# Two-layer encoder trunk on one core: twelve-tile down projections by single column groups, and the last two steps of each pair group by group

## The chip, the cores and the metric

One core of a Trainium2 chip runs the whole program. The time is that of one execution on the device in microseconds, and the lower one is the better one. TensorE (PE in the profile) multiplies, its weight loads (PEld) overlap the multiplications, VectorE (DVE) and ScalarE (ACT) do the element-wise work, GpSimd (POOL) does a little of it elsewhere in the program, and SyncE's queue (SP) issues the loads of the weights.

## The reference

256 tokens of 2048 features go through two layers. Layer 0 mixes the tokens with grouped-query attention, layer 1 with a recurrent block. Behind each mixer stands a feed-forward part, which this change is about:

```
def swiglu(h, w_gate, w_up, w_down):
    return (jax.nn.silu(h @ w_gate) * (h @ w_up)) @ w_down
...
        x = x + mix
        x = x + swiglu(rms_norm(x, norm_ffn[i]), ffn_w_gate[i], ffn_w_up[i], ffn_w_down[i])
```

`w_gate` and `w_up` are 2048 x 5632, `w_down` is 5632 x 2048, and all is float32.

## The kernel before, in words

**Products.** A float32 operand is split into a high part (`hi`, rounded to the format that TensorE takes at full rate) and a low part (`lo`, the rest). One product of tiles is three matmuls: high by high, high by low and low by high. A matmul here multiplies 128 tokens (there are two token halves, `a`) by 512 columns over 128 rows of the weights.

**Weights.** All weights of the feed-forward part stream through `load_half` (line 109): 512 KB, that is 256 rows by 512 columns, are loaded into `raw`, ScalarE casts them to `hi` (line 122) and VectorE subtracts to get `lo` (line 123). Each of the three tags has five buffers. `ffn_order` (line 137) lists the halves in the order in which TensorE takes them, and `half` (line 162) hands out the next.

**Tiles and parts.** The 5632 hidden features are 44 tiles of 128. `PARTS` (line 28) deals them out in three parts of 12, 16 and 16 tiles. For each part `ffn` (line 760) runs the units, each of which makes four hidden tiles, and then the down projection of this part, which adds to the residual `x_tok`. So a layer has 3 + 4 + 4 units and three down projections.

**Pairs.** Both are made of calls of `project_pair` (line 276). A pair computes two column groups of 512 at once, gate and up for a unit, two neighbouring groups of the output for a down projection (which so has two pairs, `c` of 0 and 2). A pair holds four accumulators, two groups by two token halves, and these are all four buffers of the pool `ps_a`. It goes through steps of two row tiles each, eight steps for sixteen tiles and six for twelve. In a plain step the first group's half is taken and multiplied (12 matmuls), then the second group's (12 matmuls).

**Seven-product steps.** Two steps of each pair, listed in `SEVEN` (line 29), use a scheme of the Strassen kind: seven products in place of eight, so 21 matmuls in place of 24. It needs sums of the weights (`seven_forms`, line 245: four VectorE additions at lines 252 to 255, a cast at 259 and a split at 260), sums of the tokens' operand (`x_forms`, line 264), four more accumulators in the pool `ps_m`, and after the last such step `merge` (line 317), which works these accumulators into two tiles `fg` and `fu`. The order of the steps is in `USUAL_STEPS` and, for the first unit of a layer, `FIRST_STEPS` (lines 30 and 31).

**After a pair.** A unit adds the accumulators to `fg` and `fu` (lines 766 and 769), applies SiLU to the gate (line 526, by way of a helper), multiplies (line 770), and `turned` (line 444) turns the result by two VectorE transposes (line 448) and sixteen ScalarE copies (line 456). The four hidden tiles are then cast and split (lines 775 and 776). A down pair adds `fg` and `fu` to `x_tok` (line 500), then the accumulators (line 509), and in the last part of layer 0 `norm.add` (line 410) then prepares the operands of the next norm, column by column (lines 412, 448, 454, 456, 404 and 405). In the last part of layer 1 the columns are stored.

**Single groups.** The output projections of attention and of the recurrence are done by `output` (line 476) and `project_tokens` (line 223): one column group at a time, two accumulators, plain steps only, one half of weights (12 matmuls, line 235) per step, and adds to `x_tok` at line 484.

**Order.** TensorE's instructions run in the order in which the program is written. Those of the other engines are ordered by a planner, which picks among what is ready by the order of the program and its own estimate of times; each engine then keeps that order.

Of the kernel before, what the change touches and what calls it, by code (L numbers as in the profile page):

```python
# [14 lines left out]
AF = mybir.ActivationFunctionType  # L15
# [10 lines left out]
NBLK = 8  # L26
DFF = 5632
PARTS = [12, 16, 16]
SEVEN = {6: (1, 3), 8: (2, 5)}
USUAL_STEPS = {6: (0, 2, 1, 4, 3, 5), 8: (0, 1, 2, 3, 4, 5, 6, 7)}  # L30
FIRST_STEPS = (0, 1, 3, 4, 2, 6, 5, 7)
HALF = 8
WIDE = 512
NCOL = D // WIDE
# [38 lines left out]
def trunk(ctx, tc, w, out):  # L73
# [56 lines left out]
    def wide(name):  # L130
        src = w[name]
        return [(src[c, i], HALF) for c in range(src.shape[0]) for i in range(src.shape[1])]

    def pair_steps(n, first=False):
        return FIRST_STEPS if first else USUAL_STEPS[n]

    def ffn_order(l):
        units = [wide(f"w_gate{l}"), wide(f"w_up{l}")]
        seq, i = [], 0
        for p, n in enumerate(PARTS):  # L140
            for _ in range(n // FOUR):
                for k in pair_steps(KT // 2, i == 0):
                    seq += [u[i + k] for u in units]
                i += KT // 2
            down = wide(f"w_down{l}_{p}")
            for c in range(0, len(down), n):
                for k in pair_steps(n // 2):
                    seq += [down[c + k], down[c + n // 2 + k]]
        return seq

    order = [(w["w_k"][i], HALF) for i in range(len(KEY_TILES))]
# [90 lines left out]
    def flat(t):  # L242
        return t.rearrange("p (k c) f -> p k (c f)", k=2)
# [29 lines left out]
        dve.tensor_tensor(t[:, 1], y[:, 4:, :], t[:, 0].bitcast(F32), ALU.subtract)  # L273
        return [(t[:, 0, i, :], t[:, 1, i, :]) for i in range(4)]

    def project_pair(xs, forms, middle, first=False):
        banks = [[new_acc() for _ in range(2)] for _ in range(2)]
        begun = set()

        def product(acc, x, wt, last=False):  # L280
            for i, (a, b) in enumerate(((x[0], wt[0]), (x[0], wt[1]), (x[1], wt[0]))):
                pe.matmul(acc, a, b, start=id(acc) not in begun, stop=last and i == 2)  # L282
# [7 lines left out]
        steps = pair_steps(len(xs) // 2, first)  # L290
        seven = [n for n in steps if n in forms]
        for n in steps:
            if n in forms:
                s1, s2, s3, s4 = forms[n]
                b11, b21, t3, b22, t1, t2, t4 = seven_forms()
                if n == seven[0]:
                    p1, q6, q5, q7 = (ps_m.tile([P, WIDE], F32, tag="pm", name=nm("pm")) for _ in range(4))
                last = n == seven[-1]
                product(p1, tokens(2 * n, 0), b11, last)
                product(banks[0][0], tokens(2 * n + 1, 0), b21)  # L300
                product(banks[1][0], s4, b22)
                product(q7, s3, t3, last)
                product(q5, s1, t1, last)
                product(q6, s2, t2, last)
                product(banks[0][1], tokens(2 * n + 1, 1), t4)
                if last:
                    middle(p1, q5, q6, q7)
            else:
                for j in range(2):
                    half()  # L310
                    hi, lo = (flat(t) for t in newest["tiles"])
                    for a in range(2):
                        for k in range(2):
                            product(banks[j][a], tokens(2 * n + k, a), (hi[:, k, :], lo[:, k, :]), n == steps[-1] and k == 1)
        return banks

# [74 lines left out]
    class Norm:  # L391
# [18 lines left out]
        def add(self, c):  # L410
            for a in range(2):
                act.activation(tmp("nj", (P, WIDE), bufs=1), x_tok[:, a, c, :], AF.Square, accum_out=self.sums[:, a, c : c + 1])
            for f in turned(x_tok[:, :, c, :]):
                self.operand(f, True)
            for n in SEVEN[KT // 2] if self.seven else ():
# [60 lines left out]
    def output(xs, norm=None, end=False, ready=0, close=None):  # L476
        for c in range(NCOL):
            accs = project_tokens(xs, ready, None if c else close)
            for a, acc in enumerate(accs):
                n = 2 if end and c == NCOL - 1 else 1  # L480
                for i in range(n):
                    sl = slice(i * WIDE // n, (i + 1) * WIDE // n)
                    y = x_tok[:, a, c, sl]
                    dve.tensor_tensor(y, y, acc[:, sl], ALU.add)
                    if end:
                        sync.dma_start(out=out[:, a, c, sl], in_=y)
            if norm is not None:
                norm.add(c)
        if norm is not None:
            norm.finish()  # L490


    def down(xs, forms, norm=None, end=False):
        for c in (0, 2):
            def middle(*banks):
                g, u = merge(*banks)
                for j, t in enumerate((g, u)):
                    for a in range(2):
                        y = x_tok[:, a, c + j, :]
                        dve.tensor_tensor(y, y, t[:, a, :], ALU.add)  # L500

            banks = project_pair(xs, forms, middle)
            for j in range(2):
                for a in range(2):
                    n = 2 if end and c + j == NCOL - 1 else 1
                    for i in range(n):
                        sl = slice(i * WIDE // n, (i + 1) * WIDE // n)
                        y = x_tok[:, a, c + j, sl]
                        dve.tensor_tensor(y, y, banks[j][a][:, sl], ALU.add)  # L509
                        if end:  # L510
                            sync.dma_start(out=out[:, a, c + j, sl], in_=y)
                if norm is not None:
                    norm.add(c + j)
        if norm is not None:
            norm.finish()

# [8 lines left out]
    def table_act(*a, **k):  # L525
        table_op(act.activation(*a, **k))
# [231 lines left out]


    def ffn(norm, nxt):  # L760
        def unit(hid, forms, seven, first):
            got = []
            banks = project_pair(norm.xs, norm.forms, lambda *banks: got.extend(merge(*banks)), first)
            g, u = got
            for a, acc in enumerate(banks[0]):
                dve.tensor_tensor(g[:, a, :], acc, g[:, a, :], ALU.add)
                table_act(g[:, a, :], g[:, a, :], AF.Silu, scale=norm.rt[:, a : a + 1])
            for a, acc in enumerate(banks[1]):
                dve.tensor_tensor(u[:, a, :], acc, u[:, a, :], ALU.add)
                dve.scalar_tensor_tensor(u[:, a, :], u[:, a, :], norm.rt[:, a : a + 1], g[:, a, :], ALU.mult, ALU.mult)  # L770
            first = len(hid)
            for f in turned(u, False):
                h = act_tile()
                hi, lo = (h[:, o : o + S].rearrange("p (q t) -> p q t", t=32) for o in (0, S))
                act.copy(hi, f)  # L775
                dve.tensor_tensor(lo, f, hi.bitcast(F32), ALU.subtract)
                hid.append(h)
            for i, n in enumerate(seven):
                if first <= 2 * n < len(hid):
                    forms[n] = x_forms(hid[2 * n], hid[2 * n + 1], f"hf{i}")  # L780

        for p, n in enumerate(PARTS):
            hid, forms = [], {}
            for i in range(n // FOUR):
                unit(hid, forms, SEVEN[n // 2], p == i == 0)
            last = p == len(PARTS) - 1
            if last and nxt is not None:
                ln_exp_tables()
            down(hid, forms, nxt if last else None, last and nxt is None)

    nr = Norm("norm_mix", KT)
    ffn(nf, nr)
# [218 lines left out]
```

## Time and profile before

| | us |
|---|---|
| median of 3 runs | 2042.35 |
| lowest and highest | 2038.47 and 2043.43 |
| profiled execution, its own time | 2042.2 |
| its span, from the first to the last instruction | 2040.4 |
| mean granted TensorE clock | 0.990 |

The profile's times are those of one execution. Its page gives busy times by engine and the costliest groups of instructions, each with the line of the kernel, the operation, the tiles written and read, the count, the busy time and mean duration, and the idle time of the engine just before them with what ended most of it. In a timeline each row has the start, the duration, the engine, the line and operation, and in brackets the idle time before it and what ended that. A row of a table of stretches has the length of the stretch, each engine's busy time with its number of instructions, the granted clock as a share, and the DMA's share and rate. In a list of waits stand the engine that waits, what it waits for, the total, how often, and the longest. A matmul's end in the profile is modelled, so that neighbouring matmuls overlap; their starts are the better measure.

### The profile page before, as it was taken

How to read it: one execution, taken by the hardware profiler on the slowest of the kernel's cores; microseconds unless marked ns; L12 is line 12 of the kernel's file. 1: busy time of each engine (PE TensorE's matmuls, PEld its weight loads, DVE VectorE, ACT ScalarE, POOL GpSimd, SP SyncE). 2: the span in 40 equal slices, each digit the busy share in tenths (PEclk: the TensorE clock that was granted, in tenths of full speed). 3: DMA queues.
4: the chain of work that ended last, by engine and by line, in shares of the span. 5: the costliest groups of instructions: out<-in, count | busy, mean ns of one | idle time of the engine just before them, and what ended most of it. 6: DMA issues, size and time to landing. Idle time of an engine off the chain costs nothing.

```text
span 2040.4 us, 27933 instructions
## 1 busy us (share of the span) xinstructions
PE 1999.7 (98%) x9920; PEld 1691.3 (83%) x9920; DVE 1721.6 (84%) x2447; ACT 1336.3 (65%) x2070; POOL 166.6 (8%) x213
## 2 busy tenths in 40 slices
PE   9999999989999999999899999999989999999999
PEld 8898888867888888888799998888768888888887
DVE  7998789877888878889868877889787889878987
ACT  7665767654667546676689987767535766457663
POOL 1563000000000000000133330000000000000000
PEclk9999999989999999999899999999999999999999
DMA  8444565555556665555646555555545566555664
GB/s 318 156 135 146 184 209 194 186 172 189 186 184 198 208 213 186 186 190 193 200 157 197 180 167 186 186 196 196 177 168 180 188 197 225 190 193 186 204 218 145
DMA packets 109004, 386.06 MB, mean 189 GB/s; under 512 B 12224, under 2 KB 12992, under 8 KB 108736
## 3 DMA queue, kind: packets, MB, share of 16 engines
q1 hardware_dynamic: 108720, 384.26, 56.9%
q8 instruction: 78, 1.28, 0.2%
q14 instruction: 62, 0.51, 0.1%
q10 hardware_dynamic: 144, 0.02, 0.0%
HBM read 382.13 MB, written 2.10 MB: 188 GB/s over the span
## 4 chain that ended last, share of the span: by engine, by line
PE 69%; DVE 17%; DMA 6%; issue 5%; ACT 3%; SPq 0%; POOL 0%; DVEq 0%; ACTq 0%
PE acc L282 38%; PE acc L235 8%; DVE lo L123 7%; PE pm L282 5%; PE acc L213 5%; DMA raw<-in_w_up_dram 4%; PE acc L328 3%; PE acc L327 3%; PE acc L329 3%; ACT tf L456 1%; DMA raw<-in_w_down_dram 1%; ACT hi L122 1%; PE pm L328 1%; PE pm L329 1%; PE pm L327 1%
## 5 line engine op out<-in xcount | busy, mean ns | idle before, releaser
L122 ACT CAST hi<-raw 128x1024 fp32r<-128x1024 f32 (+1 forms) x708 | 730.5, 1047 | 510.9 <-PE acc L282 384.7
L123 DVE TENSOR_TENSOR lo<-raw,hi 128x1024 fp32r<-128x1024 f32 (+1 forms) x708 | 855.0, 1226 | 133.4 <-ACT hi L122 129.6
L282 PE MATMUL acc<-hi,xg 128*128 128x512 f32 x2200 | 698.2, 390 | 9.8 <-DVE x_tok L509 6.0
L282 PEld LDWEIGHTS acc<-hi,xg 128*128 128x128 f32 x2200 | 413.4, 188 | 103.2 <-issue 7.8
L282 PE MATMUL acc<-lo,xg 128*128 128x512 f32 x1100 | 428.6, 390 | 0.0
L282 PE MATMUL acc<-hi,act 128*128 128x512 f32 x1072 | 349.7, 399 | 14.9 <-ACT act L775 7.5
L282 PEld LDWEIGHTS acc<-hi,act 128*128 128x128 f32 x1072 | 205.5, 192 | 65.9 <-ACT act L775 8.3
L282 PEld LDWEIGHTS acc<-lo,xg 128*128 128x128 f32 x1100 | 206.8, 188 | 42.4
L282 PE MATMUL acc<-lo,act 128*128 128x512 f32 x536 | 212.1, 396 | 0.0
L456 ACT COPY tf<-tb 32x256 f32<-32x256 f32 x448 | 181.2, 404 | 8.4 <-DVE xg L405 1.2
L235 PE MATMUL acc<-hi,act 128*128 128x512 f32 x512 | 159.8, 390 | 0.0
L327 PE MATMUL acc<-xg,hi 128*128 128x256 f32 x512 | 146.8, 287 | 3.5 <-ACT xg L404 3.4
L252 DVE TENSOR_TENSOR wx<-raw,raw 128x512 f32<-128x512 f32 x68 | 47.1, 692 | 120.0 <-DMA raw<-in_w_up_dram 89.3
L328 PE MATMUL acc<-xg,hi 128*128 128x256 f32 x512 | 146.5, 286 | 0.8 <-DVE xg L405 0.7
L329 PE MATMUL acc<-xg,lo 128*128 128x256 f32 x512 | 145.9, 285 | 0.0
L260 DVE TENSOR_TENSOR wxl<-wx,wxh 128x1536 fp32r<-128x1536 f32 x68 | 119.2, 1753 | 15.1 <-ACT wxh L259 14.8
L259 ACT CAST wxh<-wx 128x1536 fp32r<-128x1536 f32 x68 | 100.6, 1479 | 44.2 <-DVE wx L255 40.3
L213 PE MATMUL acc<-xg,hi 128*128 128x512 f32 x384 | 126.1, 396 | 0.1
L282 PEld LDWEIGHTS acc<-lo,act 128*128 128x128 f32 x536 | 103.1, 192 | 21.2
L235 PEld LDWEIGHTS acc<-hi,act 128*128 128x128 f32 x512 | 96.1, 188 | 19.6
L327 PEld LDWEIGHTS acc<-xg,hi 128*128 128x128 f32 x512 | 99.7, 195 | 3.9 <-ACT xg L404 3.9
L328 PEld LDWEIGHTS acc<-xg,hi 128*128 128x128 f32 x512 | 99.6, 195 | 1.3 <-DVE xg L405 1.3
(239 smaller groups left out, 2846.3 us busy)
## 6 DMA issues: line engine op xcount, KB each, us to landing
raw<-in_w_gate_dram SPq DMA_DIRECT2D x176, 512.0 KB, 4.4
raw<-in_w_up_dram SPq DMA_DIRECT2D x176, 512.0 KB, 4.2
raw<-in_w_down_dram SPq DMA_DIRECT2D x176, 512.0 KB, 4.3
raw<-in_w_in_dram SPq DMA_DIRECT2D x64, 512.0 KB, 4.4
raw<-in_w_qv_dram SPq DMA_DIRECT2D x40, 512.0 KB, 4.3
raw<-in_w_o_dram SPq DMA_DIRECT2D x32, 512.0 KB, 3.5
raw<-in_w_out_dram SPq DMA_DIRECT2D x32, 512.0 KB, 3.8
graw<-in_w_gates_dram SPq DMA_DIRECT2D x32, 256.0 KB, 3.5
```

The costliest lines, as they stand in the source:

```text
L122: newest["cast"] = act.copy(hi[:, sl, :], raw[:, sl, :])
L123: dve.tensor_tensor(lo[:, sl, :], raw[:, sl, :], hi[:, sl, :].bitcast(F32), ALU.subtract)
L213: pe.matmul(o, w, x, start=(k == 0 and not part), stop=(k == total - 1 and not part))
L235: pe.matmul(accs[a], x, wt[:, k, :], start=(k0 + k == 0 and n == 0), stop=(end and k == 1 and n == 2))
L252: dve.tensor_tensor(x[:, 0, :], r2[:, 0, :], r1[:, 0, :], ALU.add)
L259: act.copy(xh, x)
L260: dve.tensor_tensor(xl, x, xh[:].bitcast(F32), ALU.subtract)
L282: pe.matmul(acc, a, b, start=id(acc) not in begun, stop=last and i == 2)
L327: pe.matmul(o, hi, x[:, :S], start=start, stop=False)
L328: pe.matmul(o, hi, x[:, S:], start=False, stop=False)
L329: pe.matmul(o, lo, x[:, :S], start=False, stop=stop)
L456: act.copy(o, y)
```

## The change

The twelve-tile down projection (the first part of each layer) is no longer done in pairs but by `output`, four column groups one after the other, with plain steps in the order of the rows. Its seven-product steps, merges and the token sums for them go. The order of its loads follows. The step tables for six steps go too.

In all other pairs, units and down projections alike, the steps behind the last seven-product step are done for the first group and then for the second. For the usual order these are steps 6 and 7. For the first unit of a layer only one step is left there. What is done with a finished group is now written as a function `done`, which is called as soon as that group is complete, ahead of the second group's last steps.

The last down pair of each layer takes its steps in the order 0, 1, 3, 2, 4, 5, 6, 7.

```
-SEVEN = {6: (1, 3), 8: (2, 5)}
-USUAL_STEPS = {6: (0, 2, 1, 4, 3, 5), 8: (0, 1, 2, 3, 4, 5, 6, 7)}
+SEVEN = (2, 5)
+USUAL_STEPS = (0, 1, 2, 3, 4, 5, 6, 7)
 FIRST_STEPS = (0, 1, 3, 4, 2, 6, 5, 7)
+LAST_STEPS = (0, 1, 3, 2, 4, 5, 6, 7)
...
+    def pair_plan(steps, apart):
+        m = 1 + steps.index(SEVEN[-1]) if apart else len(steps)
+        return [(n, (0, 1)) for n in steps[:m]] + [(n, (j,)) for j in range(2) for n in steps[m:]]
+
+    def unit_steps(first):
+        return FIRST_STEPS if first else USUAL_STEPS, True
+
+    def down_steps(p, second):
+        last = p == len(PARTS) - 1
+        return LAST_STEPS if second and last else USUAL_STEPS, True
...
             down = wide(f"w_down{l}_{p}")
+            if n != KT:
+                seq += down
+                continue
             for c in range(0, len(down), n):
-                for k in pair_steps(n // 2):
-                    seq += [down[c + k], down[c + n // 2 + k]]
+                for k, cols in pair_plan(*down_steps(p, c > 0)):
+                    seq += [down[c + n // 2 * j + k] for j in cols]
...
-    def project_pair(xs, forms, middle, first=False):
+    def project_pair(xs, forms, order, middle, done):
...
-                for j in range(2):
+                for j in cols:
                     half()
                     hi, lo = (flat(t) for t in newest["tiles"])
+                    end = n == order[0][-1]
                     for a in range(2):
                         for k in range(2):
-                            product(banks[j][a], tokens(2 * n + k, a), (hi[:, k, :], lo[:, k, :]), n == steps[-1] and k == 1)
-        return banks
+                            product(banks[j][a], tokens(2 * n + k, a), (hi[:, k, :], lo[:, k, :]), end and k == 1)
+                    if end:
+                        done(j, banks[j])
...
-    def down(xs, forms, norm=None, end=False):
+    def down(xs, forms, p, norm=None, end=False):
...
-            banks = project_pair(xs, forms, middle)
-            for j in range(2):
+            def done(j, accs):
                 for a in range(2):
...
-                        dve.tensor_tensor(y, y, banks[j][a][:, sl], ALU.add)
+                        dve.tensor_tensor(y, y, accs[a][:, sl], ALU.add)
...
                 if norm is not None:
                     norm.add(c + j)
+
+            project_pair(xs, forms, down_steps(p, c > 0), middle, done)
...
+            def done(j, accs):
+                g, u = got
+                for a, acc in enumerate(accs):
+                    if j == 0:
+                        dve.tensor_tensor(g[:, a, :], acc, g[:, a, :], ALU.add)
+                        table_act(g[:, a, :], g[:, a, :], AF.Silu, scale=norm.rt[:, a : a + 1])
+                    else:
+                        dve.tensor_tensor(u[:, a, :], acc, u[:, a, :], ALU.add)
+                        dve.scalar_tensor_tensor(u[:, a, :], u[:, a, :], norm.rt[:, a : a + 1], g[:, a, :], ALU.mult, ALU.mult)
...
-            down(hid, forms, nxt if last else None, last and nxt is None)
+            if n == KT:
+                down(hid, forms, p, nxt if last else None, last and nxt is None)
+            else:
+                output(hid)
```

More of the change, by code (lines that the diff above doesn't have):

```diff
@@ L132, in wide @@
         return [(src[c, i], HALF) for c in range(src.shape[0]) for i in range(src.shape[1])]
-    def pair_steps(n, first=False):
-        return FIRST_STEPS if first else USUAL_STEPS[n]
+    def pair_plan(steps, apart):
[6 more added lines that the diff above has]
+        return LAST_STEPS if second and last else USUAL_STEPS, True
     def ffn_order(l):
@@ L141, in ffn_order @@
             for _ in range(n // FOUR):
-                for k in pair_steps(KT // 2, i == 0):
-                    seq += [u[i + k] for u in units]
+                for k, cols in pair_plan(*unit_steps(i == 0)):
+                    seq += [units[j][i + k] for j in cols]
                 i += KT // 2
             down = wide(f"w_down{l}_{p}")
+            if n != KT:
+                seq += down
+                continue
             for c in range(0, len(down), n):
-                for k in pair_steps(n // 2):
-                    seq += [down[c + k], down[c + n // 2 + k]]
+                for k, cols in pair_plan(*down_steps(p, c > 0)):
+                    seq += [down[c + n // 2 * j + k] for j in cols]
         return seq
@@ L288, in tokens @@
             return [xs[k][:, o + a * P : o + (a + 1) * P] for o in (0, S)]
-        steps = pair_steps(len(xs) // 2, first)
-        seven = [n for n in steps if n in forms]
-        for n in steps:
+        steps = pair_plan(*order)
+        seven = [n for n in order[0] if n in forms]
+        for n, cols in steps:
             if n in forms:
@@ L414, in add @@
                 self.operand(f, True)
-            for n in SEVEN[KT // 2] if self.seven else ():
+            for n in SEVEN if self.seven else ():
                 if FOUR * c <= 2 * n < FOUR * c + FOUR:
@@ L760, in ffn, with unit @@
     def ffn(norm, nxt):
-        def unit(hid, forms, seven, first):
+        def unit(hid, forms, first):
             got = []
[L763 to L770, printed above, removed]
+            def done(j, accs):
[7 more added lines that the diff above has]
+                        dve.scalar_tensor_tensor(u[:, a, :], u[:, a, :], norm.rt[:, a : a + 1], g[:, a, :], ALU.mult, ALU.mult)
+            project_pair(norm.xs, norm.forms, unit_steps(first), lambda *banks: got.extend(merge(*banks)), done)
+            u = got[1]
             first = len(hid)
@@ L777, in unit @@
                 hid.append(h)
-            for i, n in enumerate(seven):
-                if first <= 2 * n < len(hid):
+            for i, n in enumerate(SEVEN):
+                if forms is not None and first <= 2 * n < len(hid):
                     forms[n] = x_forms(hid[2 * n], hid[2 * n + 1], f"hf{i}")
         for p, n in enumerate(PARTS):
-            hid, forms = [], {}
+            hid, forms = [], {} if n == KT else None
             for i in range(n // FOUR):
-                unit(hid, forms, SEVEN[n // 2], p == i == 0)
+                unit(hid, forms, p == i == 0)
             last = p == len(PARTS) - 1
```

## The prediction, made before the changed kernel ran

> **What bounds the kernel now.** I read the page first, then TensorE's waits, then stretches of single stages, then the timeline at the places where TensorE stood.
>
> ```profile
> span 2040.4 us, 27933 instructions
> PE 1999.7 (98%) x9920; PEld 1691.3 (83%) x9920; DVE 1721.6 (84%) x2447; ACT 1336.3 (65%) x2070; POOL 166.6 (8%) x213
> ...
> L122 ACT CAST hi<-raw 128x1024 fp32r<-128x1024 f32 (+1 forms) x708 | 730.5, 1047 | 510.9 <-PE acc L282 384.7
> ```
>
> TensorE (PE) is the bound: busy 98%, and the casts of the weights (L122) mostly idle until TensorE gives a buffer back (384.7 us), so the loads run ahead of it. But 98% hides time in which matmuls run at half clock or lie wide apart. I therefore count matmuls against a pitch. The chain of waits has one undisturbed run of 512-column matmuls:
>
> ```profile
> 1231.17 87.07 PE acc L235 x384
> ```
>
> 87.07 / 384 = 0.2267 us each. The waits of TensorE in the whole span, longest first:
>
> ```profile
> PE acc L282 <- DVE x_tok L509: 11.1, 7, 2.4
> PE acc L282 <- ACT act L775: 7.5, 2, 3.8
> PE acc L282 <- DVE fg L766: 4.5, 10, 0.9
> ...
> PE pm L282 <- DVE wxl L260: 1.4, 1, 1.4
> ```
>
> The first two lie in two stretches, the twelve-tile down projection of each layer and the first step behind it: in the first 5.5 us for L509 and in the second 5.6, by the same view of these alone:
>
> ```profile
> PE acc L282 <- DVE x_tok L509: 5.5, 3, 2.4
> ...
> PE acc L282 <- DVE x_tok L509: 5.6, 4, 2.4
> ```
>
> Here are these (first two rows), the rest of the two feed-forward layers (next two), the last down pair of layer 0 and the start of the recurrence behind it:
>
> ```profile
> core 0: us, PE busy (x) PEld busy (x) DVE busy (x) ACT busy (x) POOL busy (x), PEclk, DMA share, GB/s
> 395.30:476.90 81.60, 71.60 (x290) 56.50 (x290) 68.05 (x83) 42.22 (x54) 0.00 (x0) 0.94 0.51 168
> 1445.30:1531.40 86.10, 75.62 (x294) 59.42 (x294) 69.98 (x85) 43.76 (x55) 0.00 (x0) 0.90 0.50 165
> 476.90:944.00 467.10, 465.37 (x2042) 381.99 (x2042) 394.17 (x475) 291.25 (x393) 0.00 (x0) 1.00 0.59 196
> 1531.40:2036.60 505.20, 503.72 (x2216) 414.85 (x2214) 422.39 (x506) 301.79 (x401) 0.00 (x0) 1.00 0.58 193
> 942.00:986.80 44.80, 43.30 (x189) 34.80 (x188) 44.41 (x67) 32.71 (x55) 0.00 (x0) 1.00 0.61 201
> 986.80:1004.00 17.20, 12.94 (x81) 12.00 (x81) 15.97 (x41) 14.49 (x34) 0.00 (x0) 0.80 0.42 138
> ```
>
> Length minus count times pitch is the time lost. Twelve-tile stretches: 81.60 - 290 x 0.2267 = 15.9 and 86.10 - 294 x 0.2267 = 19.4, together **35.3 us**. The other feed-forward work, some 4,258 matmuls, loses only 467.10 - 462.9 = 4.2 and 505.20 - 502.4 = 2.8, together 7.0. The last down pair loses 1.9 with VectorE (DVE) busy 44.41 of 44.80 us.
>
> The twelve-tile stretch of layer 0 on TensorE:
>
> ```profile
> 394.94 0.39 PE L282 MATMUL acc<-hi,xg 128*128 128x512 f32 x1
> 395.63 0.47 PE L282 MATMUL acc<-hi,act 128*128 128x512 f32 x1 [0.30 <-DVE fg L766]
> ...
> 411.34 0.39 PE L282 MATMUL acc<-wxh,act 128*128 128x512 f32 x1
> 415.49 0.80 PE L282 MATMUL acc<-hi,act 128*128 128x512 f32 x1 [3.76 <-ACT act L775]
> ...
> 438.59 0.50 PE L282 MATMUL acc<-hi,act 128*128 128x512 f32 x1 [2.32 <-DVE x_tok L509]
> ...
> 474.30 0.50 PE L282 MATMUL acc<-hi,xg 128*128 128x512 f32 x1 [2.40 <-DVE x_tok L509]
> ```
>
> ```profile
> 411.60:423.00 11.40, 7.20 (x19) 5.11 (x19) 6.59 (x9) 7.15 (x11) 0.00 (x0) 0.70 0.41 148
> ...
> 435.90:443.00 7.10, 4.78 (x14) 3.13 (x13) 6.76 (x10) 2.53 (x3) 0.00 (x0) 0.76 0.43 135
> ```
>
> Three stalls. **First**, step 4 of the first pair needs hidden tile 8, which the unit just ended (last matmul at 394.94) has yet to turn and cast: 3.76 us. **Second** and **third**, one step (12 matmuls) into the next pair and the next unit, the second column group's banks are not yet emptied (L509): 2.32 and 2.40 us. After the first two the granted clock falls: a mean of 0.70 over 11.40 us is 3.4 us lost, 0.76 over 7.10 is 1.7.
>
> **The change, part by part.**
>
> *Matmuls.* A twelve-tile pair has four plain steps of 24 and two seven-product steps of 21: 138, so 276 a layer. Single groups have 4 x 6 x 12 = 288. So 24 more in two layers, all on TensorE's path: 24 x 0.2267 = **+5.4 us**.
>
> *VectorE and ScalarE work removed.* Eight seven-product forms, four merges, the 16 adds of L500 and four operand forms go. I cost this at nothing of its own: it counts only through the stalls it caused. Single groups take two banks of the four and alternate, so a group's two adds have a whole group (72 x 0.2267 = 16.3 us) before their banks are wanted again. The second stall goes. The third goes too: the next unit's second pair of banks is wanted 2.7 us after the end, with two adds and perhaps one weight split before it instead of merges.
>
> *The first stall moves and grows.* In single groups tile 8 is wanted after four steps of 12, 48 x 0.2267 = 10.9 us after the stage's start, at about 406.5 in this trace's time, where the pair came to it at 411.57. When is the tile there? VectorE, then ScalarE (ACT):
>
> ```profile
> 394.80 0.68 DVE L766 TENSOR_TENSOR fg<-acc,fg 128x512 f32<-128x512 f32 x1
> 395.40 0.68 DVE L255 TENSOR_TENSOR wx<-wx,raw 128x512 f32<-128x512 f32 x1
> 396.00 0.69 DVE L766 TENSOR_TENSOR fg<-acc,fg 128x512 f32<-128x512 f32 x1
> 396.60 1.22 DVE L123 TENSOR_TENSOR lo<-raw,hi 128x1024 fp32r<-128x1024 f32 x1
> 397.73 1.28 DVE L769 TENSOR_TENSOR fu<-acc,fu 128x512 f32<-128x512 f32 x2
> 398.93 1.75 DVE L260 TENSOR_TENSOR wxl<-wx,wxh 128x1536 fp32r<-128x1536 f32 x1
> 400.59 1.41 DVE L770 SCALAR_TENSOR_TENSOR fu<-fu,nr,fg 128x512 f32<-128x512 f32 x2
> 401.92 2.36 DVE L123 TENSOR_TENSOR lo<-raw,hi 128x1024 fp32r<-128x1024 f32 x2
> 404.19 1.30 DVE L448 STREAM_TRANSPOSE tb<-fu 128x512 f32<-128x512 f32 x2
> ...
> 416.68 1.43 DVE L776 TENSOR_TENSOR act<-tf,act 128x256 fp32r<-128x256 f32 x4
> ```
>
> ```profile
> 405.52 6.65 ACT L456 COPY tf<-tb 32x256 f32<-32x256 f32 x16
> 412.19 2.94 ACT L122 CAST hi<-raw 128x1024 fp32r<-128x1024 f32 x3
> 415.04 1.32 ACT L775 CAST act<-tf 128x256 fp32r<-128x256 f32 x4
> ```
>
> The first high part is there at 415.04 + 0.33 = 415.4, the first low part at 416.68 + 0.36 = 417.0. The change takes out L260 (1.7 us of start-to-start time) and, with the gate group finished 24 matmuls (5.4 us) before the unit's end, the two gate adds and L255 ahead of the up adds (1.8 us). The weight splits and casts stay: the buffers still come free at TensorE's pace. So high 411.9, low 413.5. TensorE wants the first at 406.5 and the second two matmuls later: a wait of 5.4 and about 1 more, and then the half clock as at the first stall (3.4): some 9 us a layer, as some is covered. Lower bound: nothing of the weights between the steps, 394.94 + 0.39 (the last matmul's end) + 1.28 + 1.41 + 1.30 + 6.65 + 0.33 = 406.3, no wait. Upper bound: as late as now, 417.0 - 406.9 = 10.1 plus 3.4, 13.5. I take **9**, nearer the upper, because splits and casts stand between the steps of this chain in this trace. Stretches: 35.3 - 2 x 9 - 5.4 = **11.9 us won** (from 35.3 - 27 - 5.4 = 2.9 to 35.3 - 5.4 = 29.9).
>
> On the half clock, the Trainium skill ("TensorE: Matmul & The Clock Gate", Part 1) says that the clock drops after an idle window of some 3.4 us. The trace disagrees for short waits: the 2.32 us wait at 438.59 was followed by 0.76. By the page the two bank waits alone would not have cost clock; for a new wait of 5 us both say the same.
>
> *Pair tails.* Gate (or first column) steps 6 and 7 come before up's. The first group is finished 24 instead of 12 matmuls before the end, so its adds no longer stand at the boundary in front of the second group's. That aims at the L766 waits. Those of the first unit of a layer stay: behind its last seven-product step only one step is left, and its order is the old one. Of the 7.0 us lost elsewhere I take **5**; bounds 7 and -2 (a split of weights now behind the adds and late by one 1.22 us piece in a boundary or two). The loads change places two by two on SyncE's queue (SP); their number and size stay, and the casts that wait for TensorE hide them. If that cover went, the price would be of the size of one split, 1.22 us, a boundary.
>
> *Last pair of a layer.* Steps 3 and 2 change places, and column 2's norm work starts up to 2.7 us earlier. VectorE is full there (44.41 of 44.80), so it cannot take all of it. Matmuls of 256 columns start every 0.12 us behind it:
>
> ```profile
> 992.37 0.28 PE L328 MATMUL acc<-xg,hi 128*128 128x256 f32 x1
> 992.49 0.28 PE L329 MATMUL acc<-xg,lo 128*128 128x256 f32 x1
> ```
>
> So 17.20 - 81 x 0.12 = 7.5 us are lost there. The 1.9 us of the pair itself and a fifth of these may go: column 3's chain follows column 2's through the same buffers, so it wins no more than column 2's. I take **3.5**; bounds 8, most of the two, and -3, a form's last split (1.75) and a weight split (1.22) late. In layer 1 nothing follows but the stores, and the last group's stay last: 0.
>
> **Sum.** 11.9 + 5 + 3.5 = 20.4. Against the profiled execution's 2042.2 us (span 2040.4 plus 1.8 around it; the median of the runs shown is 2042.35): **2022 us**.
>
> **Rivals.**
>
> *Tile 8 comes nearly in time.* With VectorE freed of the forms the chain could run almost unbroken: 29.9 + 5 + 3.5 = 38.4, so 2004. For it: the minimal chain ends at 406.3 against 406.5. Against it: three weight casts went in between the copies and L775 with the copies done.
>
> *Tile 8 as late as now, and the tails give little.* 2.9 + 2 + 1, about 2036. For it: L260 was only one of the pieces in between. Against it: the gate adds do leave the front.
>
> *Slower: tile 8 later than now.* Place: the same step 4 of the first group in both layers. Each us of lateness counts twice. The sum of gains without the wait is 35.3 - 5.4 + 8.5 = 38.4, so it decides at 19.2 us a layer, that is a wait of 15.8 plus 3.4 of half clock: the tile's low part at 406.9 + 15.8 = 422.7, some 6 us later than now. Some four weight casts or splits more in the chain than now would do that; 4 us beyond it gives 2050. Against it: with TensorE standing, no buffer comes free for such casts.
>
> *The stalls were never on the path,* and only the 24 matmuls count: 2047.6. Against it: these waits are TensorE's own, in a stretch where its clock falls.
>
> **How the numbers follow.** Forecast 0.55, own range 2010 to 2032; tile in time 0.17; tile as late as now 0.16; tile later 0.08; stalls never on the path 0.04. A measurement of this kernel tells 0.3% (6.1 us) from no change, so the bounds are 2036.2 and 2048.5. Faster by more: 0.55 + 0.17 + half of 0.16 = 0.80; within: the other 0.08 + 0.04 = 0.12; slower: 0.08. The range takes in the first two rivals: 2003 to 2039.
>
> **What would show it.** Matmuls x9944; L260 x60 instead of 68; no L509 wait in the stretches; one wait for L775 in each layer, of 4 to 7 us, 48 matmuls after the stage's start, with a granted clock below 0.8 behind it; L766 waits down to those of the first units. The last down pair's wait for L260 gone. It is wrong if the L775 wait is above 10 us, if banks are waited for in single groups, or if the boundaries lose as much as now.

## The result and the profile after

The changed kernel took 2022.19 us (median of 4 runs, 2019.21 to 2022.71) where the kernel before took 2041.95 us beside it. The ratio is 0.9903 with a 95% interval of 0.9885 to 0.9920, so about 20 us less. The profiled execution took 2022.37 us.

The page of the changed kernel, whose lines have moved down by 1 to 20 (the weight cast L122 is now L123, the adds of L509 are L522, the hidden tiles' cast L775 is L795):

```profile
span 2020.6 us, 27860 instructions
PE 1995.2 (99%) x9944; PEld 1696.2 (84%) x9944; DVE 1666.0 (82%) x2347; ACT 1320.7 (65%) x2054; POOL 165.7 (8%) x213
```

TensorE has 24 matmuls more and yet 4.5 us less busy time. A matmul at half clock counts as busy for longer (0.80 us beside 0.39 in the rows of tile 8 further down), and there are fewer of these: the mean granted clock went from 0.990 to 0.993. VectorE lost 55.6 us of work. TensorE's waits in the whole span of the changed kernel (engine, line waited for, us in total, times, longest):

```profile
PE acc L247 <- ACT act L795: 5.4, 2, 2.7
PE pm L294 <- DVE wxl L272: 2.2, 1, 2.2
PE acc L342 <- DVE xg L419: 1.9, 1, 1.9
...
PE acc L294 <- DVE fg L783: 1.2, 2, 0.6
PE acc L294 <- DVE fu L786: 1.2, 4, 0.4
```

The 11.1 us for the banks (`x_tok`) are gone. The wait for the hidden tile is still there, 2.7 us once a layer. The gate's adds (L783) are waited for only in the first unit of each layer, and four short waits for the up adds (L786) have come in their place. The wait for a split of weight sums grew from 1.4 to 2.2 us.

The same stretches as before, now cut at starts of matmuls: the twelve-tile down projection of each layer with the first 24 matmuls behind it (312 matmuls), the last down pair of layer 0 (186), and the 200 matmuls behind that:

```profile
core 0: us, PE busy (x) PEld busy (x) DVE busy (x) ACT busy (x) POOL busy (x), PEclk, DMA share, GB/s
395.59:472.97 77.38, 74.14 (x313) 60.33 (x312) 45.24 (x49) 36.26 (x47) 0.00 (x0) 0.96 0.55 171
1436.98:1514.27 77.29, 74.33 (x313) 60.42 (x312) 45.24 (x49) 36.26 (x47) 0.00 (x0) 0.96 0.55 171
932.39:977.04 44.65, 42.45 (x187) 34.83 (x186) 43.91 (x67) 31.25 (x51) 0.00 (x0) 1.00 0.57 187
977.04:1016.38 39.34, 31.35 (x202) 29.45 (x200) 30.59 (x61) 26.26 (x52) 7.23 (x15) 0.83 0.51 162
```

312 matmuls at 0.2267 us take 70.7 us, so the two twelve-tile stretches lose 6.6 us each, 13.2 together. Before, cut in the same way, they took 83.90 and 87.36 us for 300 matmuls each and lost 35.2.

### The profile page after: what moved, and what is told of

Same layout as the page of the kernel before. It is cut to its first block, busy times and chain, and to the rows that moved or that the text cites. A ratio compares the mean times of both kernels' runs of the same rounds, so it can differ in the third digit from the quotient of the medians.

```text
span 2020.6 us, 27860 instructions
## 1 busy us (share of the span) xinstructions
PE 1995.2 (99%) x9944; PEld 1696.2 (84%) x9944; DVE 1666.0 (82%) x2347; ACT 1320.7 (65%) x2054; POOL 165.7 (8%) x213
## 4 chain that ended last, share of the span: by engine, by line
PE 52%; issue 41%; DVE 4%; DMA 1%; ACT 1%; POOL 0%; DVEq 0%; SPq 0%; ACTq 0%; POOLq 0%
PE acc L294 24%; PE acc L247 7%; PE acc L225 6%; PE pm L294 4%; PE acc L341 3%; PE acc L342 3%; PE acc L343 3%; DVE lo L124 2%; PE pm L342 1%; PE pm L343 1%; PE pm L341 1%; DMA raw<-in_w_up_dram 1%; ACT hi L123 0%; DMA graw<-in_w_gates_dram 0%; ACT tf L470 0%
## 5 line engine op out<-in xcount | busy, mean ns | idle before, releaser
L123 ACT CAST hi<-raw 128x1024 fp32r<-128x1024 f32 (+1 forms) x708 | 730.4, 1045 | 486.1 <-PE acc L294 314.1
L247 PE MATMUL acc<-hi,act 128*128 128x512 f32 x896 | 283.4, 395 | 6.2 <-ACT act L795 5.4
L294 PE MATMUL acc<-hi,act 128*128 128x512 f32 x800 | 252.7, 389 | 0.0
L247 PEld LDWEIGHTS acc<-hi,act 128*128 128x128 f32 x896 | 170.7, 191 | 43.8 <-ACT act L795 6.3
L294 PEld LDWEIGHTS acc<-hi,act 128*128 128x128 f32 x800 | 150.2, 188 | 32.3 <-issue 0.7
L247 PE MATMUL acc<-lo,act 128*128 128x512 f32 x448 | 176.8, 395 | 0.0
L294 PE MATMUL acc<-lo,act 128*128 128x512 f32 x400 | 155.6, 389 | 0.0
L264 DVE TENSOR_TENSOR wx<-raw,raw 128x512 f32<-128x512 f32 x60 | 41.5, 692 | 123.7 <-DMA raw<-in_w_up_dram 97.1
L271 ACT CAST wxh<-wx 128x1536 fp32r<-128x1536 f32 x60 | 88.9, 1482 | 49.6 <-DVE wx L267 46.7
L272 DVE TENSOR_TENSOR wxl<-wx,wxh 128x1536 fp32r<-128x1536 f32 x60 | 104.8, 1747 | 10.5 <-ACT wxh L271 10.5
```

What stands on the lines that cost most here:

```text
L123: newest["cast"] = act.copy(hi[:, sl, :], raw[:, sl, :])
L247: pe.matmul(accs[a], x, wt[:, k, :], start=(k0 + k == 0 and n == 0), stop=(end and k == 1 and n == 2))
L264: dve.tensor_tensor(x[:, 0, :], r2[:, 0, :], r1[:, 0, :], ALU.add)
L271: act.copy(xh, x)
L272: dve.tensor_tensor(xl, x, xh[:].bitcast(F32), ALU.subtract)
```

## The experiments

For each profile I worked out four terms. **Twelve-tile** is the time lost in the two stretches just named: their length less the count of matmuls times 0.2267 us (87.07 / 384, not rounded). **Boundaries** is the same for the 24 other units and down pairs of 186 matmuls that are neither a layer's first unit, the unit behind the twelve-tile stretch, nor the last pair. **Last pair** and **behind** are the lengths of the last two stretches. All but the times are of one execution; the times are medians, and of single executions where no number of runs stands beside them.

| kernel | twelve-tile | boundaries | last pair | behind | time |
|---|---|---|---|---|---|
| before | 35.2 | 9.4 | 44.6 | 38.3 | 2041.95 |
| changed | 13.2 | 4.5 | 44.7 | 39.3 | 2022.19 (4 runs) |
| changed, again | 13.2 | 5.7 | 46.9 | 39.2 | 2024.25 (4) |
| single groups only | 10.8 | 9.0 | 44.4 | 39.4 | 2023.72 (4) |
| single groups only, again | 10.8 | 8.3 | 44.1 | 38.9 | 2024.68 (4) |
| tails only | 30.8 | 8.0 | 45.2 | 38.7 | 2037.11 (10) |
| changed, usual order last | 12.9 | 6.1 | 44.0 | 38.7 | 2021.78 |
| changed, last pair together | 11.9 | 5.4 | 47.0 | 39.4 | 2023.53 |
| first two groups together | -0.1 | 9.9 | 45.1 | 38.1 | 2012.07 (4) |
| filled wait | 2.1 and 5.9 of filling | 4.8 | 46.7 | 37.4 | 2016.97 |
| root first | 12.8 | 6.1 | 46.3 | 36.9 | 2022.22 |
| first two together, root first, usual order | -0.1 | 5.0 | 44.2 | 38.9 | 2011.10 (4) |
| first two together, tails as before | -0.1 | 10.2 | 44.5 | 38.0 | 2014.25 (4) |

### One part alone: single groups, and tails

Single groups only (the kernel before with these lines; the token sums for these projections are not made either):

```
             down = wide(f"w_down{l}_{p}")
+            if n != KT:
+                seq += down
+                continue
...
+            if n == KT:
                 down(hid, forms, nxt if last else None, last and nxt is None)
+            else:
+                output(hid)
```

> The kernel before with one part of the change: the twelve-tile down projections by single groups; pairs end as before and the last pair keeps its order. Theory (most of the gain is the bank waits of the twelve-tile stretches that go, and the early gate adds of the pair tails shorten the wait for hidden tile 8): the stretches lose some 17 us instead of 35.3 (wait for tile 8 of 4 to 5 us and half clock, a layer), 5.4 us of matmuls are added, all else as before: about 2029. Rival 1 (the tails do nothing for tile 8): the stretches come to 13.2 us as in the changed kernel: about 2025. Rival 2 (the gain was the tails'): 2040 or more.

It took 2023.72 us, ratio 0.9924 (0.9895 to 0.9954). The waits for tile 8 sum to 5.3 us in the two layers, as in the changed kernel (5.4), so rival 1 was right on this point. The stretches lost 10.8 us, where rival 1 had 13.2: behind each wait the clock was halved for 3.4 us, in the changed kernel for 6.8. VectorE, ScalarE and then TensorE behind the unit that makes tile 8, in single groups only (its last matmul's end is at 394.39 + 0.39 = 394.78; L772 are the up adds, L451 the transposes, L778 the casts of the hidden tiles):

```profile
394.33 1.28 DVE L772 TENSOR_TENSOR fu<-acc,fu 128x512 f32<-128x512 f32 x2
395.53 1.41 DVE L773 SCALAR_TENSOR_TENSOR fu<-fu,nr,fg 128x512 f32<-128x512 f32 x2
396.85 1.22 DVE L123 TENSOR_TENSOR lo<-raw,hi 128x1024 fp32r<-128x1024 f32 x1
397.99 1.30 DVE L451 STREAM_TRANSPOSE tb<-fu 128x512 f32<-128x512 f32 x2
```

```profile
399.31 6.63 ACT L459 COPY tf<-tb 32x256 f32<-32x256 f32 x16 [0.68 <-DVE tb L451]
405.96 1.99 ACT L122 CAST hi<-raw 128x1024 fp32r<-128x1024 f32 x2
407.86 1.32 ACT L778 CAST act<-tf 128x256 fp32r<-128x256 f32 x4
```

```profile
408.31 0.50 PE L238 MATMUL acc<-hi,act 128*128 128x512 f32 x1 [2.65 <-ACT act L778]
```

The up adds start before the unit's end is reached, where before they started 2.4 us behind it, and one weight split stands ahead of the transposes instead of a split of sums and two weight splits. TensorE starts on the tile 13.5 us behind the unit's end (408.31 - 394.78), where before it was 20.2 (415.49 - 395.33). With the tails (changed kernel) it is 13.6.

Tails only (the changed kernel, twelve-tile projections in pairs as before):

```
-            if n != KT:
-                seq += down
-                continue
...
-            if n == KT:
-                down(hid, forms, p, nxt if last else None, last and nxt is None)
-            else:
-                output(hid)
+            down(hid, forms, p, nxt if last else None, last and nxt is None)
```

> The changed kernel with the twelve-tile down projections in pairs with seven-product steps, as before; tails group by group and the last pair's order as changed. Theory: boundaries win 4.8 us as in the changed kernel, the last pair and the start of the recurrence lose about 1, and in the twelve-tile stretches only tile 8 comes 2 us earlier in each layer, bank waits stay: 2034 to 2038. Rival (the tails also cure the bank waits there, since fewer adds stand at the boundary): below 2030.

2037.11 us, ratio 0.9981 (0.9972 to 0.9991): some 3 to 4 us less, and the theory's range. TensorE's waits:

```profile
PE acc L295 <- DVE x_tok L523: 13.5, 9, 2.7
PE acc L295 <- ACT act L796: 7.6, 2, 3.9
PE acc L295 <- DVE fu L787: 2.9, 7, 0.7
```

Bank waits (13.5 us, 11.8 of them in the two stretches) and the tile's wait (7.6) are as long as before (11.1 and 7.5). That the stretches lose 4.4 us less in this profile is the clock. In layer 1 it was 0.98, where the kernel before had 0.90:

```profile
1445.21:1527.79 82.58, 71.36 (x302) 56.79 (x301) 70.48 (x85) 43.36 (x54) 0.00 (x0) 0.98 0.54 174
```

So nearly all of the gain is the single groups'.

### The last pair

Usual order: `LAST_STEPS = USUAL_STEPS` in the changed kernel.

> The changed kernel with the usual order of steps in the last down pair of each layer. Theory (VectorE is full in that pair, so the order only chooses which seven-product step is late): the wait for the sums' low part goes from step 2's to another step and stays between 1 and 3 us; time from the pair's start to 200 matmuls into the recurrence within 1.5 us of the changed kernel's 83.99. Rival (the new order itself made the step late): no such wait, 2 us or more shorter.

Together: the last pair of a layer is not taken apart.

```
-        return LAST_STEPS if second and last else USUAL_STEPS, True
+        return LAST_STEPS if second and last else USUAL_STEPS, not (second and last)
```

> The changed kernel with the last down pair of each layer ending as before, both groups in each step (its new order of steps kept). Theory (column 3's norm work follows column 2's through the same buffers and VectorE is full): the time from the pair's start to 200 matmuls into the recurrence is within 1.5 us of the changed kernel's 83.99. Rival 1 (the early norm work is worth what it starts earlier): 2 to 3 us longer. Rival 2 (it gets in the way): 2 us or more shorter.

The stretches in the usual order:

```profile
934.01:977.99 43.98, 42.78 (x188) 34.76 (x186) 43.56 (x66) 30.85 (x49) 0.00 (x0) 1.00 0.58 194
977.99:1016.71 38.72, 29.90 (x202) 28.04 (x200) 29.11 (x62) 27.61 (x54) 8.01 (x15) 0.82 0.52 167
```

and with the groups together:

```profile
931.52:978.48 46.96, 44.37 (x188) 35.95 (x186) 44.61 (x67) 31.65 (x52) 0.00 (x0) 0.96 0.57 185
978.48:1017.88 39.40, 31.45 (x202) 29.48 (x200) 30.66 (x62) 26.65 (x53) 7.21 (x15) 0.83 0.55 160
```

In the usual order the sum is 82.7, within the theory's 1.5 of 83.99; the wait did become smaller, two of 1.2 us in all, so the rival had a part of it right. TensorE waits for column 2's operands 3.45 and 0.85 us in this run, as before (3.45 and 0.66), although the two groups end apart. With the groups together the sum is 86.4, what rival 1 asked for, but not for its reason: behind the pair the time is the changed kernel's, 39.40 against 39.34. What is longer is the pair, and its clock is 0.96, so a half clock fell in it. The changed kernel's second profile shows the same with the groups apart:

```profile
931.88:978.83 46.95, 44.36 (x188) 35.90 (x187) 45.13 (x68) 32.67 (x54) 0.00 (x0) 0.96 0.56 184
```

Over the table, the seven profiles with the new order have 44.7 to 47.0 us for the pair, the six with the old one 44.0 to 44.6. The wait of 2.2 to 2.3 us that the new order makes is followed by half clock in four of the seven, and over pair and start of the recurrence together the order wins nothing.

Root first: in the changed kernel the norm's root is worked out ahead of the last column's turning.

```
-        def add(self, c):
+        def add(self, c, root=False):
...
+            if root:
+                self.finish()
             for f in turned(x_tok[:, :, c, :]):
...
-        if norm is not None:
-            norm.finish()
```

> The changed kernel with the norm's root in front of layer 1 worked out right behind the squares of the last column, ahead of this column's turning and casts. Theory (the early norm work of column 2 is given back because the root, 14.6 us behind the pair's end, now comes last: TensorE waits 1.1 us for it and again for the recurrence's first operands): the wait for the root's diagonal is gone and the time from the last pair's start to 200 matmuls into the recurrence is 2 to 4 us shorter than 83.99. Rival (the casts of the weights and column 3's chain set the end): within 1 us of 83.99.

TensorE's wait for the root's diagonal is gone and the time behind the pair is 36.94 us, the lowest of all. But others with the same order of steps lie between 37.4 and 39.4, the pair itself had a half clock again (46.3), and the sum of 83.28 is the rival's. The first 96 matmuls behind the pair, which use the operands of all four columns, show more. For the kernel before, the changed one and root first in turn, here are the 72 up to column 3's first operand and the 24 from there:

```profile
986.86:1002.60 15.74, 11.61 (x74) 10.91 (x72) 14.51 (x38) 13.32 (x31) 0.00 (x0) 0.78 0.45 150
1002.60:1005.98 3.38, 3.24 (x25) 3.05 (x26) 2.09 (x5) 2.40 (x5) 0.20 (x4) 1.00 0.05 18
```

```profile
977.04:990.58 13.54, 10.63 (x73) 10.01 (x72) 12.79 (x30) 12.21 (x28) 0.00 (x0) 0.87 0.52 166
990.58:996.83 6.25, 5.04 (x24) 4.63 (x25) 2.54 (x9) 2.28 (x8) 0.33 (x5) 0.73 0.35 115
```

```profile
978.10:991.38 13.28, 9.15 (x74) 8.75 (x72) 12.85 (x33) 12.12 (x29) 0.00 (x0) 1.00 0.53 167
991.38:996.38 5.00, 4.86 (x25) 4.50 (x25) 2.47 (x7) 2.46 (x5) 0.20 (x4) 0.66 0.33 92
```

Column 3's first operand is reached at the same time in the last two (13.54 and 13.28 us), and the 24 matmuls behind it take 6.25 and 5.00 us, with 1.7 us lost to half clock in each (0.27 of 6.25, 0.34 of 5.00). So the root's place is worth some 1.2 us there. What it is worth in the whole time stays open, since the clock moves more than that.

### The wait for tile 8, and the half clock

First two groups together (`SIX_STEPS` is 0 to 5; steps 0 to 3 for both groups, then 4 and 5 for each):

```
-        m = 1 + steps.index(SEVEN[-1]) if apart else len(steps)
+        m = 4 if len(steps) == 6 else 1 + steps.index(SEVEN[-1]) if apart else len(steps)
...
-                output(hid)
+                project_pair(hid, {}, (SIX_STEPS, True), None, added)
+                output(hid, begin=2)
```

> The changed kernel, but in the twelve-tile down projection the first two column groups go through steps 0 to 3 together, then each through steps 4 and 5; groups 3 and 4 singly as in the changed kernel. Same matmuls; hidden tile 8 is wanted 96 matmuls (21.8 us) after the stage's start instead of 48 (10.9). Theory (what is left of loss in these stretches is the wait for tile 8 and the half clock behind it, and the tile is there 13.5 to 15 us after the unit): no wait for it, 13.2 us less in the two layers, about 2009. Rival 1 (the tile is late whenever TensorE comes, as the casts of the weights that TensorE frees stand in its way): a wait of 2 us or more stays, 2015 to 2022. Rival 2 (bank waits come back with four banks taken at once): waits for x_tok, 2015 or more.

The twelve-tile stretch of layer 0 (that of layer 1 has the same length and clock):

```profile
394.91:465.63 70.72, 70.72 (x313) 58.56 (x312) 44.24 (x49) 36.18 (x47) 0.00 (x0) 1.00 0.60 186
```

Nothing is lost there any more, as the theory had it, and the bank waits of rival 2 did not come. The whole took 2012.07 us, ratio to before 0.9854 (0.9834 to 0.9873): 10 us below the changed kernel, not 13. The boundaries lost 9.9 us in this profile, 5.4 more than in the changed kernel's; why is not shown.

Filled wait: 13 matmuls whose product is not used, ahead of step 4 of the first group.

```
+            if k0 == 8:
+                for i in range(fill):
+                    pe.matmul(spare, xs[7][:, :P], xs[6], start=True, stop=True)
             half()
```

> The changed kernel with 13 more matmuls (2.9 us), whose product is not used, just ahead of step 4 of the first group of the twelve-tile down projections, on tiles that are long there. Theory (the half clock behind the wait comes from TensorE standing, and costs 3.3 us a layer): the wait for tile 8 is filled and the clock stays full: 5 to 7 us less than the changed kernel. Rival (the clock falls for another reason, or TensorE is the later one): the same time or up to 6 us more.

2016.97 us in one execution, 5.4 less than the changed kernel's profiled one and below all eight of that kernel (2019.21 to 2025.98), though it does 26 matmuls more. Its stretches:

```profile
395.32:470.06 74.74, 73.99 (x327) 60.86 (x325) 44.44 (x49) 36.28 (x47) 0.00 (x0) 1.00 0.57 177
1434.60:1509.36 74.76, 74.02 (x327) 60.85 (x326) 44.45 (x49) 36.28 (x47) 0.00 (x0) 1.00 0.60 176
```

The clock stays at 1.00, and each stretch is 2.6 us shorter than the changed kernel's 77.3. In the other kernels with single groups 13 of the 14 waits for tile 8 were followed by half clock. So the half clock comes from TensorE standing, and it is worth keeping TensorE at work during a wait.

### What the boundaries are worth

> The changed kernel once more, unaltered, for a second profile. Theory (the loss at the boundaries of the pairs depends on when loads land and differs from one execution to the next, so one profile's 4.5 us says little): boundaries outside the twelve-tile stretches between 3 and 10 us in this profile, the twelve-tile stretches within 0.5 of 13.2, the time near 2022. Rival (the boundaries are set by the order of instructions): 4.5 again, within 0.5.

> Single groups alone once more, beside the changed kernel on one chip. Theory (the pair tails and the last pair's order together are worth 0 to 3 us on top of single groups): 2022 to 2025. Rival (they are worth what the boundary term said, 5 us and more): 2027 or more.

First two groups together, with the tails and the last pair's order as before the change:

> First two column groups of the twelve-tile down projection together, then single groups, and all other pairs ending as before, in the usual order. Theory (the tails are worth 0 to 3 us): 2011 to 2015, beside 2012 with the tails. Rival (the tails are worth 5): 2017 or more.

The changed kernel took 2024.25 us (ratio 0.9918, 0.9903 to 0.9934), single groups only 2024.68 (0.9923, 0.9905 to 0.9940) and the third 2014.25 (0.9871, 0.9851 to 0.9891). The boundaries of the changed kernel's second profile lose 5.7 us, not 4.5. Over the table, nine profiles with the tails lose 4.5 to 9.9, on average 6.2; four without lose 8.3 to 10.2, on average 9.2. The tails win some 3 us there on average, though the two ranges overlap. The times were in the ranges of both theories, 0 to 3 us for the tails, and don't show a gain on top of single groups: the intervals of the changed kernel and of single groups only overlap almost wholly.

The best of all, first two groups together with the root first and the usual order (no change of what is computed), took 2011.10 us, ratio to before 0.9849 (0.9832 to 0.9867). It was expected so:

> The two before put together (first two groups together; root first), with the usual order of steps in the last pair. If both theories hold and add up: 13.2 + 3 us less than the changed kernel, about 2006. If only the first holds: about 2008.

That is 2011, not 2006 to 2008. The root's place adds nothing to it that these runs can tell. With the usual order TensorE did not wait for the root's diagonal in the first place.

## Why the prediction was right, step by step

**Matmuls: right.** 24 more, 5.4 us, all paid.

**Bank waits: right.** None is left in single groups or in the unit behind them, and tails only shows that they were not the tails' to cure.

**Tile 8: right in kind, but the wait came out half as long, and for a reason that was half wrong.** I forecast a wait of 5.4 us and about 1 more, and 9 us lost a layer. The changed kernel shows:

```profile
406.25 0.39 PE L247 MATMUL acc<-hi,act 128*128 128x512 f32 x1
409.34 0.51 PE L247 MATMUL acc<-hi,act 128*128 128x512 f32 x1 [2.71 <-ACT act L795]
409.68 0.60 PE L247 MATMUL acc<-lo,act 128*128 128x512 f32 x1
410.82 0.80 PE L247 MATMUL acc<-hi,act 128*128 128x512 f32 x1 [0.54 <-DVE act L796]
```

The high part is waited for until 409.34 (2.7 us, below the 4 to 7 that I had named as a sign) and the low part until 410.82. From 409.70 on TensorE runs at half clock, and 6.6 us are lost. The chain ahead of it:

```profile
395.34 1.28 DVE L786 TENSOR_TENSOR fu<-acc,fu 128x512 f32<-128x512 f32 x2
396.54 1.41 DVE L787 SCALAR_TENSOR_TENSOR fu<-fu,nr,fg 128x512 f32<-128x512 f32 x2
397.87 1.22 DVE L124 TENSOR_TENSOR lo<-raw,hi 128x1024 fp32r<-128x1024 f32 x1
399.00 1.30 DVE L462 STREAM_TRANSPOSE tb<-fu 128x512 f32<-128x512 f32 x2
```

```profile
400.33 6.63 ACT L470 COPY tf<-tb 32x256 f32<-32x256 f32 x16 [0.72 <-DVE tb L462]
406.99 1.99 ACT L123 CAST hi<-raw 128x1024 fp32r<-128x1024 f32 x2
408.89 1.32 ACT L795 CAST act<-tf 128x256 fp32r<-128x256 f32 x4
```

The step that was mis-sized said that the weight splits and casts stay as they were, and took out only L260, the two gate adds and L255. In fact the up adds came at once, without the weight split that had stood between the unit's end and them, one weight split went from between the multiplication and the transposes, and two casts instead of three stood behind the copies. These two splits of 1.2 us and the cast of 1.0 are about what the forecast was late by: TensorE starts on the tile 13.6 us behind the unit's end (409.34 - 395.76), where I had 16.6 (411.9 - 395.33). I gave 1.8 us of it to the tails; single groups only, whose gate adds come 2.5 us later than the changed kernel's, has the tile at the same time. So it came with the single groups. Whether the forms taken off VectorE or the changed order of the loads did it, no run separates. The stretches won 35.2 - 13.2 - 5.4 = 16.6 us where I had 11.9.

**Half clock.** I had 3.4 us for it a layer. The second run of single groups only shows what that hides. The same wait stands in both layers of it (2.8 us from start to start beyond the pitch), and behind one the clock was halved for 6.8 us and behind the other not at all:

```profile
395.48:473.01 77.53, 74.13 (x313) 60.47 (x312) 45.19 (x49) 36.25 (x47) 0.00 (x0) 0.96 0.56 170
1437.99:1512.70 74.71, 71.29 (x313) 58.40 (x312) 45.14 (x49) 36.26 (x47) 0.00 (x0) 1.00 0.57 177
```

The stretches lose 6.8 and 4.0 us. The Trainium skill ("TensorE: Matmul & The Clock Gate", Part 1) says that the window that is watched runs freely. By this the same wait can fall in different places of it, which agrees with these two rows. The idle window of some 3.4 us that the Trainium skill has in the same part is not borne out as a least length: waits of 2.7 us were followed by half clock in most of the profiles, in the changed kernel before the second, shorter wait had ended, and the single wait of 2.2 to 2.3 us in the last pair was in four of seven.

**Pair tails: 5 us forecast, 4.9 in the first profile, about 3 over all.** That the gate adds leave the boundary is shown (their waits are down to those of the first units), but up adds that come late (L786) took a part of the place, and between executions this term moves by more than it is worth.

**Last pair of a layer: wrong, -3.5 forecast, +1.1 measured.** The step that failed said that column 2, being finished earlier, would have its norm work done earlier, and that this would carry through to the recurrence. Column 2's operands did come earlier: the waits for them went from 3.4 us (L404) and 0.7 (L405) to 1.9 (L419). But the new order of steps did that and not the early finish: with the groups apart in the usual order the 72 matmuls take 15.86 us (before 15.74), with the groups together in the new order 13.63 (changed 13.54). Over all profiles they take 15.7 to 15.9 us in the usual order and 13.1 to 13.6 in the new one. And the norm's root came later. In the changed kernel, on ScalarE and TensorE:

```profile
990.02 1.71 ACT L418 ACTIVATE xg<-tf,pk 128x256 fp32r<-128x256 f32 x4 [0.38 <-DVE tf L468]
991.63 0.19 ACT L541 ACTIVATE rsq_s<-nrt 128x2 f32<-128x2 f32 x1
```

```profile
993.09 1.00 PE L450 MATMUL pm<-ndg,ones 128*128 128x128 f32 x4 [1.08 <-DVE ndg L444]
```

and in the kernel before:

```profile
997.52 0.20 ACT L526 ACTIVATE rsq_s<-nrt 128x2 f32<-128x2 f32 x1 [0.16 <-DVE nrt L423]
```

The root starts 991.63 - 977.04 = 14.6 us behind the pair's end, where before it was 997.52 - 986.86 = 10.7. It stands behind column 3's casts now, and TensorE waits 1.1 us for its diagonal (`ndg`, with which it spreads the root over the partitions), which it did not before. With 1.7 us of half clock in the same 24 matmuls (6.25 us against 3.38) this takes back more than the 2.2 us by which TensorE is earlier at column 3's first operand. The new order, which I had counted on for the 1.9 us of the pair, moved the wait there to the earlier seven-product step and made it longer, 2.2 us instead of 1.4, where I had said that it would go.

That the sum was right to a microsecond was luck, since two errors met: the stretches won 4.7 us more than forecast, the last pair with what is behind it 4.6 us less.

**The rivals.** Tile 8 in time did not happen in this change, but the first two groups together made it so, and that won 10 us. Tile 8 as late as now did not come, nor later: it came 6.6 us earlier. That the stalls were never on the path is refuted: the matmuls grew by 5.4 us and the time fell by 20.

## What to carry to other kernels

Work taken off an engine that is not the bottleneck pays where a chain behind it ends in a wait of the bottleneck: here 24 more matmuls, 5.4 us, bought off 22 us of waits and half clock. When a stage is made to start on a fresh result sooner, count how many instructions stand ahead of the first use; doing two column groups side by side for the first steps put 48 more matmuls there, and nothing was lost in those stretches. A stall of the matrix engine costs its length and often some half clock, so count matmuls against their pitch instead of trusting a busy share.

## What the runs showed of the hardware that was not expected

Useless matmuls in a wait made the kernel faster: 26 of them, 5.9 us of work, took the profiled execution from 2022.37 to 2016.97 us. The two stretches account for 5.2 us of it, because the clock stayed at 1.00 there.

After the same wait of 2.7 us the granted clock was halved for 6.8 us, for 3.4 us or not at all. One such stretch of the changed kernel and one of single groups only:

```profile
409.70:416.50 6.80, 6.26 (x15) 4.46 (x14) 3.20 (x6) 2.46 (x4) 0.00 (x0) 0.50 0.66 228
```

```profile
409.70:413.12 3.42, 3.33 (x8) 2.65 (x9) 2.18 (x5) 0.43 (x1) 0.00 (x0) 0.50 0.94 297
```

In the first, 15 matmuls stand in 6.80 us, with a wait of 0.5 us among them, where at full clock 30 go into it.
